# Fox queries and keys and the convolution's input turned by VectorE squares and memory, branches taken mixer by mixer, in a decoder layer on one Trainium2 core

## The chip, the core and the metric

The kernel runs on one core of one Trainium2 chip. The metric is device time in microseconds, the median of three runs. Engines are named as in the profile: PE (TensorE, matrix products; PEld is its weight load), DVE (VectorE), ACT (ScalarE), POOL (GpSimd), SP (SyncE). Transfers are issued from SP's queue (weights and other loads) and from POOL's (everything written to memory and read back).

## The reference, cut

One decoder layer over 256 tokens of 2048 channels in float32. One input product feeds three mixers; each mixer's output is multiplied by a weight matrix and by a gate, and the three are summed.

```python
u = rms_norm(x, attn_norm)
proj = einsum('bsd,de->bse', u, w_in)                    # 2048 -> 14424 columns
fq, fk, fv, ff, cq, ckv, kpe, gqkv, gz, gb, ga, gate = split(proj)
o_fox = fox_mixer(fq, fk, fv, ff, fox_fgate_bias)        # 8 heads of 128, causal, c_t - c_s on the logits
o_mla = mla_mixer(cq, ckv, kpe, ...)                     # 8 heads
def gdn_mixer(qkv, z, b_logit, a_logit, conv_w, ...):
    qkv_c = silu(causal_depthwise_conv(qkv, conv_w))     # 4 taps along the tokens, 3072 channels
    q, k, v = split(qkv_c); q, k = l2_norm(heads(q)), l2_norm(heads(k))
    o = gated_delta_rule_chunked(q, k, v, g, beta)       # a triangular solve in each chunk of 64
    return rms_norm(o, out_norm) * silu(z)
gates = sigmoid(gate)                                    # 3 x 2048 columns
merged = sum(gates[b] * einsum('bsc,cd->bsd', o[b], w_branch[b]) for b in range(3))   # fox, mla, gdn
x = x + einsum('bsd,de->bse', merged, w_out)
h = rms_norm(x, mlp_norm)
x = x + einsum('bsf,fd->bsd', square(relu(einsum('bsd,df->bsf', h, w_up))), w_down)
return rms_norm(x, final_norm)
```

## The kernel before

**Products.** `gemm` (L237) streams each weight matrix once, in steps. In a step SP loads two blocks of 128 rows by 512 columns into `raw` (four buffers), ACT rounds them to `wh` (L253), DVE forms the remainder `wl` (L254; three buffers each), and PE runs 12 matmuls (L260 to L262: two row blocks, two halves of the tokens, three products of high and low parts). A block of 512 output columns takes 8 steps where 2048 rows are summed, 4 in a branch (1024 rows). Where `evac` is called, the finished PSUM pair `mm` is read out, scaled by `scaled_evac` on ACT and DVE by turns.

**Order.** Each engine runs its instructions in the order written. `weave` runs one piece of a side generator behind every step: the mixers' own work is written as generators with `yield`s. `behind` keeps such a piece after the step's `wh` and `wl`. `later(k, f)` runs `f` k steps on; `tick` counts the steps. So a piece that waits holds up the next `wh` on ACT or the next `wl` on DVE, and through them PE.

**Two ways of turning.** A product needs its left operand with channels on partitions, and PSUM results have tokens there. Fox queries and keys (`fox_evac`, tile `ft`, L621) and the convolution's input (`gqkv_evac`, tile `cv`, L697) are transposed by PE into PSUM, 4 transposes of 128 by 128 for each half of the tokens and 512 columns. Then ACT and DVE copy `ft` to `fqT` and `fkT`; the convolution reads `cv` directly (one ACT operation L699 and three DVE operations L701 for each 128 channels). The branches' sum, the residual and the MLP's hidden layer instead go through `turned` (L1060 to L1065): two DVE transposes of 32 by 32 squares, one DMA that writes `turn` to memory, four that read it back permuted into `zy`, all five on POOL's queue, the four behind a wait for the first; TURN steps later ACT and DVE form high and low parts (`halves_of`, L1074 and L1075; behind w_out `gained`, L1124, ahead of them).

**Stages.** Latents; fox columns (six blocks) with the mla mixer woven in; the fox mixer; convolution columns (six blocks) with the delta rule's decays; the gate columns (96 steps) with the rest of the delta rule; the branches; w_out; four chunks of w_up and w_down. The forget gate's chain (softplus on DVE, tiles `sfp` and `nl`) ends in the small product `fc` (L640), followed by the mla products `bf` (L503 to L505). The delta rule's decay matrix `E` is read back from memory in one DMA (L1002's queue), worked on at L777 to L779, and multiplied with products `pg` into `AT` and `E` (L828 to L832). Its triangular solve runs on DVE in 31 rounds (tile `fs`, L853 and L855), goes to memory as `td`, comes back in eight DMAs as `DT`, is transposed by DVE into `D` (L878), and feeds small matmuls `pO` and `pD` (L886). In the branches the loop runs over four blocks n of 512 columns, and in each over the mixers in the order gdn, fox, mla; the sum `acc` of each n is turned at once. `load_x2` loads the residual at the start of w_out.

Of the kernel before, what the change touches and what calls it, by code (L numbers as in the profile page):

```python
# [11 lines left out]
F32 = mybir.dt.float32  # L12
# [6 lines left out]
P = 128  # L19
# [15 lines left out]
TURN = 9  # L35
# [22 lines left out]
def decoder_kernel(ctx: ExitStack, tc: tile.TileContext, x, attn_norm, w_in, fox_fgate_bias, mla_q_norm,  # L58
# [279 lines left out]
    def ev_copy(o, i):  # L338
        evc[0] += 1
        if evc[0] % 2:  # L340
            A.copy(out=o, in_=i)
        else:
            V.tensor_copy(out=o, in_=i)

# [263 lines left out]
    fv = big("fv").rearrange("p (t c) -> p t c", t=2)  # L608

# [3 lines left out]
    def fox_evac(bi, t, ps):  # L613
        if bi >= 4:
            scaled_evac(fv[:, t, (bi - 4) * 512:(bi - 3) * 512], ps, t)
            return
        e = me("fe")
        scaled_evac(e, ps, t)
        pt = psx("ft").rearrange("p (a t) -> p a t", a=4)
        for a in range(4):  # L620
            PE.transpose(pt[:, a, :], e[:, a * P:(a + 1) * P], ident)  # L621
        h0 = (bi % 2) * 4
        if bi < 2:
            A.activation(out=fqT[:, h0:h0 + 4, t * P:(t + 1) * P], in_=pt, func=AF.Copy, scale=-(HD ** -0.5))
        else:
            ev_copy(fkT[:, h0:h0 + 4, t * P:(t + 1) * P], pt)
# [58 lines left out]
    def gqkv_evac(bi, t, ps):  # L685
        e = me("gq")
        scaled_evac(e, ps, t)
        gx[t] = e
        if t == 0:
            return  # L690
        for a in range(2):
            pt = psx("cv").rearrange("p (a b) -> p a b", a=2)
            y = t2("y").rearrange("p (a b) -> p a b", a=2)
            for b in range(2):
                c = 2 * a + b
                for tt in range(2):
                    PE.transpose(pt[:, b, tt * P:(tt + 1) * P], gx[tt][:, c * P:(c + 1) * P], ident)  # L697
                ct = bi * 4 + c
                A.activation(out=y[:, b, :], in_=pt[:, b, :], func=AF.Copy, scale=cw[:, 72 + ct:73 + ct])  # L699
                for d in range(1, 4):  # L700
                    V.scalar_tensor_tensor(out=y[:, b, d:], in0=pt[:, b, 0:S - d],  # L701
                                           scalar=cw[:, (3 - d) * 24 + ct:(3 - d) * 24 + ct + 1],
                                           in1=y[:, b, d:], op0=ALU.mult, op1=ALU.add)
            ct = bi * 4 + 2 * a
            if ct < 16:
                h = ct % 8
                A.activation(out=kq[h // 4][:, h % 4:h % 4 + 2, 1 - ct // 8, :], in_=y, func=AF.Silu)
            else:
# [22 lines left out]
    def gdn():  # L731
# [53 lines left out]
        yield "decays"  # L785

# [257 lines left out]

    o_b = [[], [], o_gdn]
    again = [reload(spilled["fox"], "of", o_b[0]), reload(spilled["mla"], "om", o_b[1])]
    weave(gates(0, 12), chain(delta, *again))
    run(delta)

    def turned(src, then):

        zy = big("zy")
        z, y = zy[:, 0:1024], zy[:, 1024:2048]
        zv = z.rearrange("p (j t k b) -> p t k j b", j=4, t=2, k=4)
        for t in range(2):
            V.transpose(out=zv[:, t], in_=src[t].rearrange("p (k j b) -> p k j b", k=4, j=4))  # L1060
        d = dp.tile([P, 1024], F32, tag="turn", name=nm("turn"), bufs=4)
        nc.gpsimd.dma_start(out=d, in_=z)  # L1062
        dv = d.rearrange("(g a) (j x) -> j a g x", a=32, j=4)
        for j in range(4):
            nc.gpsimd.dma_start(out=y[32 * j:32 * j + 32].rearrange("a (g x) -> a g x", g=4), in_=dv[j])  # L1065
        later(TURN, lambda: then(y))

# [10 lines left out]
    for n in range(4):  # L1078
        acc = [t2("acc") for _ in range(2)]
        for i, b in enumerate((2, 0, 1)):  # L1080
# [4 lines left out]
            def evac(bi, t, ps, n=n, acc=acc, i=i, gt=gt):  # L1085
                g = gt[t]
                if i == 0:
                    V.tensor_tensor(out=acc[t], in0=ps, in1=g, op=ALU.mult)
                else:
                    V.tensor_tensor(out=g, in0=ps, in1=g, op=ALU.mult)  # L1090
                    V.tensor_tensor(out=acc[t], in0=acc[t], in1=g, op=ALU.add)
                if i == 2 and t == 1:
                    turned(acc, lambda y: halves_of(y, n, mHt, mLt))

            if n == 0 and b < 2:
                run(again[b])
            weave(gemm(by_tile(lambda k, b=b: o_b[b][0][:, k, :]), by_tile(lambda k, b=b: o_b[b][1][:, k, :]), w_branch[0, b], 0, 8,
                       [(n * 512, 512)], evac), chain(*again))
# [127 lines left out]
```

## Time and profile before

| | us |
|---|---|
| time, median of 3 runs | 1696.25 (1693.98 to 1700.75) |
| time of the profiled execution | 1696.24 |
| its span | 1694.5 |
| PE busy | 1672.8 (99%) |
| DVE busy | 1027.7 (61%) |
| ACT busy | 807.7 (48%) |
| POOL busy | 113.2 (7%) |

The profiled execution takes 1.7 us more than its span. PE is busy nearly throughout; its matmuls are pipelined, so busy does not mean at full rate, and time is also lost where they follow each other more slowly than elsewhere. Over the span the core moves 210 GB/s.

### The profile page before, as it was taken

How to read it: one execution, taken by the hardware profiler on the slowest of the kernel's cores; microseconds unless marked ns; L12 is line 12 of the kernel's file. 1: busy time of each engine (PE TensorE's matmuls, PEld its weight loads, DVE VectorE, ACT ScalarE, POOL GpSimd, SP SyncE). 2: the span in 40 equal slices, each digit the busy share in tenths (PEclk: the TensorE clock that was granted, in tenths of full speed). 3: DMA queues.
4: the chain of work that ended last, by engine and by line, in shares of the span. 5: the costliest groups of instructions: out<-in, count | busy, mean ns of one | idle time of the engine just before them, and what ended most of it. 6: DMA issues, size and time to landing. Idle time of an engine off the chain costs nothing.

```text
span 1694.5 us, 21459 instructions
## 1 busy us (share of the span) xinstructions
PE 1672.8 (99%) x7987; PEld 1403.8 (83%) x7987; DVE 1027.7 (61%) x1418; ACT 807.7 (48%) x1029; POOL 113.2 (7%) x202
## 2 busy tenths in 40 slices
PE   9999999999999999999999999999999999999997
PEld 9888889978788788888888778888888888888886
DVE  5746446676668845746675656555665556556655
ACT  6545436555646433544444554434443344434443
POOL 0000000000011100001210111100110011001100
PEclk9999999999999999999999999999999999999999
DMA  7755564766557755877888787856885687668863
GB/s 239 204 149 186 162 176 131 229 188 186 165 171 217 212 155 146 274 220 239 276 290 262 234 237 237 251 196 190 245 267 194 196 238 241 198 194 232 243 207 138
DMA packets 190761, 356.52 MB, mean 210 GB/s; under 512 B 17945, under 2 KB 38849, under 8 KB 190145
## 3 DMA queue, kind: packets, MB, share of 16 engines
q1 hardware_dynamic: 177040, 311.33, 60.7%
q0 software_dynamic: 13296, 43.29, 8.4%
q8 instruction: 62, 1.02, 0.2%
q10 hardware_dynamic: 320, 0.53, 0.1%
q14 instruction: 43, 0.34, 0.1%
HBM read 331.50 MB, written 23.61 MB: 210 GB/s over the span
## 4 chain that ended last, share of the span: by engine, by line
PE 93%; DMA 3%; DVE 2%; issue 1%; ACT 1%; POOL 0%; SPq 0%; DVEq 0%; POOLq 0%; ACTq 0%
PE mm L261 28%; PE mm L262 27%; PE mm L260 27%; DVE wl L254 1%; DMA raw<-in_w_in_dram 1%; DMA E<-gcd 1%; DMA raw<-in_w_up_dram 1%; PE bf L503 0%; PE bf L504 0%; PE bf L505 0%; PE mm L1188 0%; PE mm L1187 0%; PE mm L1186 0%; PE po L419 0%; PE pg L828 0%
## 5 line engine op out<-in xcount | busy, mean ns | idle before, releaser
L254 DVE TENSOR_TENSOR wl<-raw,wh 128x1024 fp32r<-128x1024 f32 (+3 forms) x552 | 663.4, 1203 | 542.7 <-ACT wh L253 539.9
L253 ACT CAST wh<-raw 128x1024 fp32r<-128x1024 f32 (+3 forms) x552 | 571.5, 1037 | 707.7 <-PE mm L262 647.6
L261 PE MATMUL mm<-wl,uH 128*128 128x512 f32 (+3 forms) x896 | 345.7, 386 | 1.6 <-DVE wl L254 1.6
L262 PE MATMUL mm<-wh,uL 128*128 128x512 f32 (+3 forms) x896 | 343.4, 383 | 0.0
L260 PE MATMUL mm<-wh,uH 128*128 128x512 f32 (+3 forms) x896 | 319.4, 387 | 2.6 <-ACT wh L253 2.6
L261 PE MATMUL mm<-wl,hH 128*128 128x512 f32 x512 | 199.4, 389 | 1.0 <-DVE wl L254 1.0
L262 PE MATMUL mm<-wh,hL 128*128 128x512 f32 x512 | 199.2, 389 | 0.0
L261 PEld LDWEIGHTS mm<-wl,uH 128*128 128x128 f32 x896 | 169.1, 189 | 33.2 <-DVE wl L254 3.6
L260 PEld LDWEIGHTS mm<-wh,uH 128*128 128x128 f32 x896 | 168.1, 189 | 32.9 <-ACT wh L253 3.1
L262 PEld LDWEIGHTS mm<-wh,uL 128*128 128x128 f32 x896 | 169.1, 189 | 29.6
L261 PE MATMUL mm<-wl,dH 128*128 128x512 f32 x480 | 186.7, 389 | 0.0
L262 PE MATMUL mm<-wh,dL 128*128 128x512 f32 x480 | 186.7, 389 | 0.0
L260 PE MATMUL mm<-wh,hH 128*128 128x512 f32 x512 | 178.5, 389 | 0.2 <-ACT wh L253 0.2
L260 PE MATMUL mm<-wh,dH 128*128 128x512 f32 x480 | 167.2, 389 | 0.0
L261 PEld LDWEIGHTS mm<-wl,hH 128*128 128x128 f32 x512 | 96.1, 188 | 21.8 <-DVE wl L254 1.9
L260 PEld LDWEIGHTS mm<-wh,hH 128*128 128x128 f32 x512 | 96.0, 188 | 20.5 <-ACT wh L253 0.6
L262 PEld LDWEIGHTS mm<-wh,hL 128*128 128x128 f32 x512 | 96.1, 188 | 19.9
L262 PEld LDWEIGHTS mm<-wh,dL 128*128 128x128 f32 x480 | 90.1, 188 | 18.7
L261 PEld LDWEIGHTS mm<-wl,dH 128*128 128x128 f32 x480 | 90.1, 188 | 18.7
L260 PEld LDWEIGHTS mm<-wh,dH 128*128 128x128 f32 x480 | 90.1, 188 | 18.7
L1065 POOL DMA_DIRECT2D zy<-turn x96 | 52.4, 553 | 104.7 <-DMA turn<-zy 31.5
L1062 POOL DMA_DIRECT2D turn<-zy x24 | 13.3, 556 | 643.0 <-DVE zy L1060 643.0
(419 smaller groups left out, 1754.5 us busy)
## 6 DMA issues: line engine op xcount, KB each, us to landing
raw<-in_w_in_dram SPq DMA_DIRECT2D x192, 512.0 KB, 4.0
raw<-in_w_up_dram SPq DMA_DIRECT2D x128, 512.0 KB, 4.3
raw<-in_w_down_dram SPq DMA_DIRECT2D x128, 512.0 KB, 4.4
raw<-in_w_branch_dram SPq DMA_DIRECT2D x48, 512.0 KB, 4.8
raw<-in_w_out_dram SPq DMA_DIRECT2D x32, 512.0 KB, 5.8
turn<-zy POOLq DMA_DIRECT2D x24, 512.0 KB, 3.3
zy<-turn POOLq DMA_DIRECT2D x96, 128.0 KB, 6.0
gd<-ge POOLq DMA_DIRECT2D x24, 256.0 KB, 4.7
```

The source lines that it names most:

```text
L253: h = A.copy(out=wh[:, :, :n], in_=raw[:, :, :n])
L254: l = V.tensor_tensor(out=wl[:, :, :n], in0=raw[:, :, :n], in1=wh[:, :, :n].bitcast(F32), op=ALU.subtract)
L260: PE.matmul(ps[t][:, :n], lhsT=lhsH(k, t), rhs=wh[:, kk, :n], start=(k == 0), stop=False)
L261: PE.matmul(ps[t][:, :n], lhsT=lhsH(k, t), rhs=wl[:, kk, :n], start=False, stop=False)
L262: PE.matmul(ps[t][:, :n], lhsT=lhsL(k, t), rhs=wh[:, kk, :n], start=False, stop=last)
L1062: nc.gpsimd.dma_start(out=d, in_=z)
L1065: nc.gpsimd.dma_start(out=y[32 * j:32 * j + 32].rearrange("a (g x) -> a g x", g=4), in_=dv[j])
```

## The change

The fox queries and keys and the convolution's input now go through `turned`, ten more groups of it; the 80 PE transposes `ft` and `cv` and their copies out of PSUM are gone. `turned` takes several functions, run on successive steps from step TURN on (8 instead of 9): for fox two `fox_heads` on ACT, for the convolution `by_channel` (two copies into `ch`) and two halves of `conv`, which now reads memory tile `ch` instead of PSUM. `tick` no longer keeps the first-in order of what is due. The delta rule waits 11 more steps behind its decays, and the reloads of the fox and mla outputs run beside it from step 80 on instead of behind it. The branches' outer loop is now over the mixers (fox, mla, gdn), the inner one over n; `acc` is one tile for all columns, and only the gdn pass turns it.

```diff
-TURN = 9
+TURN = 8
@@ tick
-        while pending and pending[0][0] <= 0:
+        due = [p for p in pending if p[0] <= 0]
+        pending[:] = [p for p in pending if p[0] > 0]
+        for p in due:
             with behind():
-                pending.pop(0)[1]()
+                p[1]()
@@ turned, moved up from behind the gates, and used by all
-    def turned(src, then):
+    def turned(src, *then, delay=TURN):
         zy = big("zy")
...
-        later(TURN, lambda: then(y))
+        for i, f in enumerate(then):
+            later(delay + i, lambda f=f: f(y))
@@ fox_evac
-        e = me("fe")
+        e = fe[t] = me("fe")
         scaled_evac(e, ps, t)
-        pt = psx("ft").rearrange("p (a t) -> p a t", a=4)
-        for a in range(4):
-            PE.transpose(pt[:, a, :], e[:, a * P:(a + 1) * P], ident)
+        if t == 1:
+            turned([fe[0], fe[1]], *[lambda y, t=t: fox_heads(bi, y, t) for t in range(2)])
+
+    def fox_heads(bi, y, t):
         h0 = (bi % 2) * 4
-        if bi < 2:
-            A.activation(out=fqT[:, h0:h0 + 4, t * P:(t + 1) * P], in_=pt, func=AF.Copy, scale=-(HD ** -0.5))
-        else:
-            ev_copy(fkT[:, h0:h0 + 4, t * P:(t + 1) * P], pt)
+        d = (fqT if bi < 2 else fkT)[:, h0:h0 + 4, t * P:(t + 1) * P].rearrange("p k (g b) -> p k g b", b=32)
+        yt = y.rearrange("p (g t k b) -> p t k g b", g=4, t=2, k=4)[:, t]
+        A.activation(out=d, in_=yt, func=AF.Copy, scale=-(HD ** -0.5) if bi < 2 else 1.0)
@@ gqkv_evac
-        for a in range(2):
-            pt = psx("cv").rearrange("p (a b) -> p a b", a=2)
...
-                    PE.transpose(pt[:, b, tt * P:(tt + 1) * P], gx[tt][:, c * P:(c + 1) * P], ident)
...
+        turned([gx[0], gx[1]], lambda y: by_channel(y, bi), lambda y: conv(y, bi, 0), lambda y: conv(y, bi, 1))
+
+    def by_channel(y, bi):
+        u = chans[bi] = big("ch")[:, 0:1024].rearrange("p (k t) -> p k t", k=4)
+        yv = y.rearrange("p (g t k b) -> p t k g b", g=4, t=2, k=4)
+        for t in range(2):
+            ev_copy(u[:, :, t * P:(t + 1) * P].rearrange("p k (g b) -> p k g b", b=32), yv[:, t])
+
+    def conv(_, bi, a):
...
@@ gdn, behind the decays
         yield "decays"
+        for _ in wait(11):
+            yield
@@ gates and branches
-    weave(gates(0, 12), chain(delta, *again))
-    run(delta)
+    mixers = both(delta, chain(idle(80), *again))
+    weave(gates(0, 12), mixers)
+    run(again[0])
...
-    for n in range(4):
-        acc = [t2("acc") for _ in range(2)]
-        for i, b in enumerate((2, 0, 1)):
+    acc = [big("acc") for _ in range(2)]
+    for b in range(3):
+        if b == 1:
+            run(again[1])
+        if b == 2:
+            run(mixers)
+        for n in range(4):
...
-                if i == 2 and t == 1:
-                    turned(acc, lambda y: halves_of(y, n, mHt, mLt))
+                if b == 2 and t == 1:
+                    turned([acc[tt][:, n * 512:(n + 1) * 512] for tt in range(2)], lambda y: halves_of(y, n, mHt, mLt))
...
-                       [(n * 512, 512)], evac), chain(*again))
+                       [(n * 512, 512)], evac), mixers)
```

Where the instructions stand now is shown at three places. `wl` of successive steps tell the steps apart.

**DVE, end of the triangular solve, before:** `NT` is the solve's result, from which `td` is written to memory, and `D` is the transposes of `DT`, which comes back.

```order
L855 TENSOR_REDUCE NT_939_4510<-fs_952_4589 128x16
L254 TENSOR_TENSOR wl_1068_5275<-raw_1066_5272,wh_1067_5274 128x1024
L254 TENSOR_TENSOR wl_1075_5301<-raw_1073_5298,wh_1074_5300 128x1024
L254 TENSOR_TENSOR wl_1080_5325<-raw_1078_5322,wh_1079_5324 128x1024
L878 STREAM_TRANSPOSE D_1076_5316<-DT_1042_5134 32x16x32 x2
L254 TENSOR_TENSOR wl_1083_5343<-raw_1081_5340,wh_1082_5342 128x1024
L878 STREAM_TRANSPOSE D_1076_5316<-DT_1042_5134 32x16x32
L254 TENSOR_TENSOR wl_1088_5397<-raw_1086_5394,wh_1087_5396 128x1024
```

After, the same place:

```order
L888 TENSOR_REDUCE NT_982_4724<-fs_999_4811 128x16
L256 TENSOR_TENSOR wl_1086_5333<-raw_1084_5330,wh_1085_5332 128x1024
L256 TENSOR_TENSOR wl_1090_5355<-raw_1088_5352,wh_1089_5354 128x1024
L256 TENSOR_TENSOR wl_1093_5373<-raw_1091_5370,wh_1092_5372 128x1024
L256 TENSOR_TENSOR wl_1096_5399<-raw_1094_5396,wh_1095_5398 128x1024
L256 TENSOR_TENSOR wl_1099_5417<-raw_1097_5414,wh_1098_5416 128x1024
L256 TENSOR_TENSOR wl_1102_5435<-raw_1100_5432,wh_1101_5434 128x1024
L256 TENSOR_TENSOR wl_1109_5461<-raw_1107_5458,wh_1108_5460 128x1024
L256 TENSOR_TENSOR wl_1112_5479<-raw_1110_5476,wh_1111_5478 128x1024
L256 TENSOR_TENSOR wl_1115_5497<-raw_1113_5494,wh_1114_5496 128x1024
L256 TENSOR_TENSOR wl_1118_5515<-raw_1116_5512,wh_1117_5514 128x1024
L911 STREAM_TRANSPOSE D_1119_5530<-DT_1087_5350 32x16x32 x3
```

Three `wl` stood between the solve and `D`, now there are ten.

**DVE, the branches' sum, before:** the `zy` transposes of n=0, and the low halves `mL` that read what comes back; `gate` and `acc` are the read-out of the next products.

```order
L1060 STREAM_TRANSPOSE zy_1385_6946<-acc_1335_6700 128x4x4x32
L1060 STREAM_TRANSPOSE zy_1385_6946<-acc_1336_6701 128x4x4x32
L254 TENSOR_TENSOR wl_1404_7020<-raw_1402_7017,wh_1403_7019 128x1024
L254 TENSOR_TENSOR wl_1411_7046<-raw_1409_7043,wh_1410_7045 128x1024
L254 TENSOR_TENSOR wl_1414_7064<-raw_1412_7061,wh_1413_7063 128x1024
L1088 TENSOR_TENSOR acc_1387_6955<-mm_1391_6961,gate_1389_6957 128x512
L1088 TENSOR_TENSOR acc_1388_6956<-mm_1392_6962,gate_1390_6958 128x512
L254 TENSOR_TENSOR wl_1417_7082<-raw_1415_7079,wh_1416_7081 128x1024
L254 TENSOR_TENSOR wl_1420_7100<-raw_1418_7097,wh_1419_7099 128x1024
L254 TENSOR_TENSOR wl_1427_7128<-raw_1425_7125,wh_1426_7127 128x1024
L1075 TENSOR_TENSOR mL_1333_6698<-zy_1385_6946,mH_1331_6696 128x4x128 x2
```

After, in the gdn pass (the two `zy` transposes of n=0 stand just above the first row; those of n=1 are among the rows):

```order
L256 TENSOR_TENSOR wl_1504_7512<-raw_1502_7509,wh_1503_7511 128x1024
L256 TENSOR_TENSOR wl_1513_7549<-raw_1511_7546,wh_1512_7548 128x1024
L256 TENSOR_TENSOR wl_1516_7567<-raw_1514_7564,wh_1515_7566 128x1024
L1123 TENSOR_TENSOR gate_1489_7449<-mm_1491_7453,gate_1489_7449 128x512
L1123 TENSOR_TENSOR gate_1490_7450<-mm_1492_7454,gate_1490_7450 128x512
L1124 TENSOR_TENSOR acc_1341_6708<-acc_1341_6708,gate_1489_7449 128x512
L1124 TENSOR_TENSOR acc_1342_6709<-acc_1342_6709,gate_1490_7450 128x512
L256 TENSOR_TENSOR wl_1519_7585<-raw_1517_7582,wh_1518_7584 128x1024
L356 STREAM_TRANSPOSE zy_1505_7531<-acc_1341_6708 128x4x4x32
L356 STREAM_TRANSPOSE zy_1505_7531<-acc_1342_6709 128x4x4x32
L256 TENSOR_TENSOR wl_1522_7603<-raw_1520_7600,wh_1521_7602 128x1024
L1103 TENSOR_TENSOR mL_1339_6706<-zy_1487_7440,mH_1337_6704 128x4x128 x2
```

Six `wl` stood between `zy` and `mL`, now five, and the next group's `zy` stands ahead of them. ACT's cast `mH` of the same group stands at the same step.

**ACT, end of w_out and start of w_up, before:** `wh` casts, and `gcol`, the scaling of what comes back from memory for the third block of columns (n=2).

```order
L253 CAST wh_1665_8380<-raw_1664_8378 128x1024
L253 CAST wh_1695_8443<-raw_1694_8441 128x1024
L1124 ACTIVATE zy_1639_8233<-zy_1639_8233,gcol_92 128x8x32 x4
L253 CAST wh_1698_8469<-raw_1697_8467 128x1024
L253 CAST wh_1701_8487<-raw_1700_8485 128x1024
L1116 ACTIVATE junk_1667_8397,ss2_1550_7738<-xx0_1543_7732 128x512
L1074 CAST hH_1546_7735<-zy_1639_8233 128x4x128 x2
```

After:

```order
L255 CAST wh_1662_8364<-raw_1661_8362 128x1024
L255 CAST wh_1665_8382<-raw_1664_8380 128x1024
L1155 ACTIVATE zy_1639_8243<-zy_1639_8243,gcol_92 128x8x32 x4
L255 CAST wh_1695_8453<-raw_1694_8451 128x1024
L1102 CAST hH_1546_7733<-zy_1639_8243 128x4x128 x2
L255 CAST wh_1698_8471<-raw_1697_8469 128x1024
```

The scaling of n=2 stood behind the first cast of w_up, now it stands behind the last cast of w_out, one step earlier.

## Rows read from the trace of the kernel before

**Rows 1.** Of the page: busy time of each engine with its share of the span and its instructions, and the chain that ended last, its shares by engine:

```profile
PE 1672.8 (99%) x7987; PEld 1403.8 (83%) x7987; DVE 1027.7 (61%) x1418; ACT 807.7 (48%) x1029; POOL 113.2 (7%) x202
...
PE 93%; DMA 3%; DVE 2%; issue 1%; ACT 1%; POOL 0%; SPq 0%; DVEq 0%; POOLq 0%; ACTq 0%
```

**Rows 2.** What TensorE waited for, over the whole span: engine, line and releaser, us in total, times, longest us:

```profile
PE fc L640 <- issue: 2.8, 1, 2.8
...
PE pO L886 <- DVE D L878: 0.7, 1, 0.7
```

**Rows 3.** Five stretches of the span: us, then busy us and (instructions) of each engine, granted TensorE clock as a share of full speed, busy share of the DMA engines, GB/s:

```profile
84.00:92.00 8.00, 5.23 (x33) 5.02 (x32) 3.72 (x12) 3.35 (x7) 0.00 (x0) 0.79 0.46 134
356.00:376.00 20.00, 16.27 (x70) 12.27 (x69) 14.55 (x35) 11.46 (x16) 0.00 (x0) 1.00 0.54 175
584.00:611.00 27.00, 25.90 (x235) 20.56 (x234) 11.12 (x12) 9.28 (x11) 5.60 (x10) 0.87 0.65 198
700.00:825.00 125.00, 125.00 (x553) 103.42 (x552) 71.06 (x72) 56.94 (x61) 14.58 (x27) 1.00 0.80 250
960.00:1000.00 40.00, 37.74 (x162) 29.80 (x161) 23.65 (x38) 21.57 (x34) 5.47 (x10) 1.00 0.70 210
```

**Rows 4.** The two groups of TensorE transposes, over the span (count, duration in ns min/median/max, first and last start), a piece of one of them in the chain of work (start us, us, what), and one of the four-matmul pieces of `pg`, which the sum needs further on:

```profile
L697 PE MATMUL cv<-cst,gq x48: 270/272/328, 346.6 to 525.9; 128*128 128x128 f32 x48
...
L621 PE MATMUL ft<-cst,fe x32: 270/272/417, 87.5 to 221.5; 128*128 128x128 f32 x32
...
163.19 0.87 PE ft L621 x8
...
500.96 0.86 PE pg L828 x4
```

**Rows 5.** The chain of work around the forget gate's prefix sum `fc`: start us, us, what:

```profile
84.31 2.75 issue
...
87.65 1.24 PE ft L621 x8
...
88.89 0.21 PE bf L503
```

**Rows 6.** VectorE's groups over the span, shapes apart: line, operation, out<-in, shapes, count | busy us, mean ns of one | idle time before them and its releaser:

```profile
L254 DVE TENSOR_TENSOR wl<-raw,wh 128x1024 fp32r<-128x1024 f32 x520 | 635.1, 1223 | 517.4 <-ACT wh L253 516.7 <-DMA om<-om_d 0.3
...
L1060 DVE STREAM_TRANSPOSE zy<-acc 128x512 f32<-128x512 f32 x8 | 5.2, 689 | 0.0
...
L701 DVE SCALAR_TENSOR_TENSOR y<-cv,cw,y 128x255 f32<-128x255 f32 x24 | 11.0, 478 | 2.4 <-ACT y L699 2.3
...
L830 DVE TENSOR_TENSOR AT<-pg,E 128x256 f32<-128x256 f32 x8 | 3.3, 420 | 1.6 <-PE pg L828 1.5
...
L832 DVE SCALAR_TENSOR_TENSOR E<-pg,ns,E 128x128 f32<-128x128 f32 x16 | 4.8, 345 | 0.2
...
L175 DVE TENSOR_TENSOR rnt<-rnt,rnh 128x32 f32<-128x32 f32 x3 | 0.6, 186 | 0.0
```

**Rows 7.** The chain of work where the delta rule's `DT` is made and its first small matmuls run (start us, us, what); the last line is VectorE's waits of 584 to 611 us:

```profile
580.55 3.92 DMA td<-NT
...
585.65 4.18 DMA DT<-td
...
594.65 0.43 PE mm L261
...
608.14 0.43 PE mm L262
...
DVE D L878 <- DMA DT<-td: 5.5, 1, 5.5
```

**Rows 8.** The chain of work where `E` is read back (start us, us, what), and TensorE's instructions behind it (start us, us, instruction, idle before it and releaser):

```profile
352.31 9.02 DMA E<-gcd
...
365.52 0.74 PE L260 MATMUL mm<-wh,uH 128*128 128x512 f32 x2 [2.65 <-ACT wh L253]
```

**Rows 9.** ScalarE's instructions at the end of the w_out product: start us, us, instruction, idle before it and releaser:

```profile
962.32 1.71 ACT L1124 ACTIVATE zy<-zy,gcol 128x256 f32<-128x256 f32 x4 [3.37 <-DMA zy<-turn]
...
986.75 1.71 ACT L1124 ACTIVATE zy<-zy,gcol 128x256 f32<-128x256 f32 x4 [4.52 <-DMA zy<-turn]
```

**Rows 10.** GpSimd's DMA issues in the branches and at the start of w_out (start us, us, instruction, idle before it and releaser), and, last, the SyncE issues of the residual `xx`:

```profile
869.94 0.54 POOL L1062 DMA_DIRECT2D turn<-zy  x1 [19.13 <-DVE zy L1060]
...
874.74 2.21 POOL L1065 DMA_DIRECT2D zy<-turn  x4 [4.26 <-DMA turn<-zy]
...
902.58 0.54 POOL L1062 DMA_DIRECT2D turn<-zy  x1 [23.48 <-DVE zy L1060]
...
911.38 2.21 POOL L1065 DMA_DIRECT2D zy<-turn  x4 [8.26 <-issue]
...
945.16 0.56 POOL L1062 DMA_DIRECT2D turn<-zy  x1
...
955.70 1.10 POOL L1065 DMA_DIRECT2D zy<-turn  x2 [2.10 <-issue]
...
898.16 4.55 SPq L1106 DMA_DIRECT2D xx<-in_x_dram  x6
```

**Rows 11.** Of the page, DMA issues: out<-in, queue, count, KB each, median us from issue to landing:

```profile
turn<-zy POOLq DMA_DIRECT2D x24, 512.0 KB, 3.3
...
zy<-turn POOLq DMA_DIRECT2D x96, 128.0 KB, 6.0
```

More of the change, by code (lines that the diff above doesn't have):

```diff
@@ L343, in ev_copy @@
             V.tensor_copy(out=o, in_=i)
+    def turned(src, *then, delay=TURN):
+        zy = big("zy")
+        z, y = zy[:, 0:1024], zy[:, 1024:2048]
+        zv = z.rearrange("p (j t k b) -> p t k j b", j=4, t=2, k=4)
+        for t in range(2):
+            V.transpose(out=zv[:, t], in_=src[t].rearrange("p (k j b) -> p k j b", k=4, j=4))
+        d = dp.tile([P, 1024], F32, tag="turn", name=nm("turn"), bufs=4)
+        nc.gpsimd.dma_start(out=d, in_=z)
+        dv = d.rearrange("(g a) (j x) -> j a g x", a=32, j=4)
+        for j in range(4):
+            nc.gpsimd.dma_start(out=y[32 * j:32 * j + 32].rearrange("a (g x) -> a g x", g=4), in_=dv[j])
+        for i, f in enumerate(then):
+            later(delay + i, lambda f=f: f(y))
     cw_r = cp.tile([96, P], F32, tag="cw_r", name="cw_r")
@@ L608, in decoder_kernel @@
     fv = big("fv").rearrange("p (t c) -> p t c", t=2)
+    fe = {}
     def fox_evac_at(b0):
@@ new lines, in gqkv_evac @@
+        turned([gx[0], gx[1]], lambda y: by_channel(y, bi), lambda y: conv(y, bi, 0), lambda y: conv(y, bi, 1))
+    chans = {}
+    def by_channel(y, bi):
+        u = chans[bi] = big("ch")[:, 0:1024].rearrange("p (k t) -> p k t", k=4)
+        yv = y.rearrange("p (g t k b) -> p t k g b", g=4, t=2, k=4)
+        for t in range(2):
+            ev_copy(u[:, :, t * P:(t + 1) * P].rearrange("p k (g b) -> p k g b", b=32), yv[:, t])
+    def conv(_, bi, a):
+        u = chans[bi]
+        y = t2("y").rearrange("p (a b) -> p a b", a=2)
+        for b in range(2):
+            c = 2 * a + b
+            ct = bi * 4 + c
+            A.activation(out=y[:, b, :], in_=u[:, c, :], func=AF.Copy, scale=cw[:, 72 + ct:73 + ct])
+            for d in range(1, 4):
+                V.scalar_tensor_tensor(out=y[:, b, d:], in0=u[:, c, 0:S - d],
+                                       scalar=cw[:, (3 - d) * 24 + ct:(3 - d) * 24 + ct + 1],
+                                       in1=y[:, b, d:], op0=ALU.mult, op1=ALU.add)
+        ct = bi * 4 + 2 * a
+        if ct < 16:
+            h = ct % 8
+            A.activation(out=kq[h // 4][:, h % 4:h % 4 + 2, 1 - ct // 8, :], in_=y, func=AF.Silu)
+        else:
+            h = ct - 16
+            A.activation(out=y, in_=y, func=AF.Silu)
+            pb = psx("vb").rearrange("p (t b d) -> p t b d", t=2, b=2)
+            for tt in range(2):
+                for b in range(2):
+                    PE.transpose(pb[:, tt, b, :], y[:, b, tt * P:(tt + 1) * P], ident)
+            ev_copy(vtok[:, :, h * P:(h + 2) * P], pb.rearrange("p t b d -> p t (b d)"))
@@ L1043, in reload, with idle, both @@
                 yield
+    def idle(n):
+        for _ in wait(n):
+            yield
+    def both(*gens):
+        gens = list(gens)
+        while gens:
+            gens = [g for g in gens if next(g, gens) is not gens]
+            yield
     o_b = [[], [], o_gdn]
     again = [reload(spilled["fox"], "of", o_b[0]), reload(spilled["mla"], "om", o_b[1])]
-    weave(gates(0, 12), chain(delta, *again))
-    run(delta)
-    def turned(src, then):
[L1056 to L1065, printed above, removed]
-        later(TURN, lambda: then(y))
+    mixers = both(delta, chain(idle(80), *again))
+    weave(gates(0, 12), mixers)
+    run(again[0])
     def halves_of(y, n, H, L):
```

33 lines of the change are left out of this document (5 added, 28 removed).

## The prediction

> **What bounds the kernel now.** I read the busy times first: PE is busy for 1672.8 of 1694.5 us and makes up 93% of the chain that ended last [rows 1]. The list of what PE waited for holds little, its largest entry 2.8 us ahead of `fc` [rows 2]. So I looked for time that PE loses without being listed, by stretches. From 700 to 825 us it runs 553 matmuls in 125 us, 0.226 us each, so a step of 12 takes 2.71 us: PE at full rate [rows 3]. Four stretches fall short: 84 to 92 (idle 2.8), 356 to 376 (idle 3.7), 584 to 611 (idle 1.1, granted clock 0.87) and 960 to 1000, where 162 matmuls should take 36.6 us and take 40 [rows 3]. A change pays if it takes work off PE or shortens one of these, and it costs if it makes a fifth. The other engines have room on the whole (DVE 61%) [rows 1]. Only their local order can stop PE: `wl` runs ahead of PE by its three buffers, some two steps or 5.4 us.
>
> **PE's work that goes.** The 80 transposes have the same duration in both groups, median 272 ns, but that is latency: eight of them take 0.87 us in the chain, 0.109 each [rows 4]. The first eight of `ft` belong to `fc`, below. The other 72 are worth **−7.8 us**, since PE bounds where they stand.
> [...]
>
> **The stretch at `fc`.** PE waits 2.75 us, then runs eight `ft` (1.24 us), and `bf` starts at 88.89 [rows 5]. The wait ends with DVE's softplus chain. The two new transposes of the fox block, 0.689 us each [rows 6], stand in that chain, so `fc` comes at least 1.4 us later, and up to 2.1 if the remainders that change places there also come first. The 1.24 us go. So `bf` starts 0.2 to 0.9 us later: **+0.6**.
>
> **The triangular solve.** Of `td`'s 3.92 us and `DT`'s 4.18 us, DVE waited 5.5 us ahead of `D` [rows 7]; the `wl` behind it were late for PE. [...] The half clock comes in two stretches, matmuls of 0.43 us around 594 (behind the wait) and around 608 (behind `pD`'s small matmuls) [rows 7]. The first stretch and the idle time, 1.75 + 1.1, belong to the wait. Now ten steps, 27 us, lie between the solve and `D` instead of three, against some 9.3 us of transfers. So **−2.9**; nothing if another transfer delays `DT`, −4.6 if the second stretch goes too.
>
> **The stretch at `E`.** `E` takes 9.02 us to come back and PE idles 2.65 us behind it [rows 8]. This chain stays. There are ten `cv` transposes less for PE ahead of it, 1.1 us, which lengthen the wait, and some convolution operations (0.478 us each [rows 6]) less on DVE within it. The turn of the first convolution block is queued behind `E` on POOL, so `ch` may be late. I take **0**, between −1.5 and +2.
>
> **The convolution's last block on DVE.** Its halves ran right behind its product; now they come six to eight steps later, among the norm (16 small operations of 0.186), `AT` (0.420) and `E` (0.345) [rows 6]. Between four `wl` I count on DVE: 4 `wl` 4.9, norm 3.0, six `AT` 2.5, ten `E` 3.5, a copy 0.7 (as a transpose), ten convolution operations 4.8; together 19.4 us. PE has four steps, 10.8, and two pieces `pg` of 0.86 [rows 4], 12.6 in all. The excess of 6.8 against a lead of 5.4 leaves 1.4 late; as the steps ahead are full too, the lead is not whole. **+2**, between 0 and +4. Convolution operations read memory now instead of PSUM; I keep their price, and half of it would end this term.
>
> **The end of w_out.** ACT waits twice for `zy` there, 3.37 and 4.52 us [rows 9]. The second wait, n=2, moves one step earlier, ahead of a cast that was hidden; what it waits for starts no earlier. **+2.7**, one step; 0 if `zy` lands a step earlier.
>
> **The branches.** In the gdn pass a block is turned every 4 steps instead of 12, and what comes back must be there in 5 steps instead of 6: 13.6 us instead of 16.3, plus what ACT is ahead, at most half a us by my estimate. A chain from the issue of `turn` to the last landing, with the median 6.0 us of `zy` [rows 11], took 13.0 us at 869.94 and 17.0 at 902.58, when the residual's loads ran at 898.16 to 902.71; one that overlapped another took 17.6 from 945.16 [rows 10]. Before, all fitted, as PE lost nothing from 700 to 825. Now the residual's loads meet the third block: about 3 us late for it, others hardly. **+2**, between 0 and +8.
>
> **What costs nothing.** Ten more groups of `turned` put 20 × 0.689 = 13.8 us on DVE, spread over 300 us in which PE is the bound; 50 more DMA issues go to POOL, busy 7%. The fox blocks wait eight, then six steps, more than a chain of 13. The `acc` reads and sums are as many as before. If that cover fails, one late chain costs what it is late, 1 to 4 us.
>
> **Sum.** −7.8 + 0.6 − 2.9 + 0 + 2 + 2.7 + 2 = −3.4 us. The profiled execution took 1696.24, the median of runs is 1696.25, so the difference carries over: **1692.8 us**. What a measurement of this kernel can tell from no change is about 0.5%, 8.5 us: faster means under 1687.8, slower over 1704.7.
>
> **Rivals.**
> *All covers hold:* no new wait in the convolution, w_out and branches. −7.8 + 0.2 − 2.9 = −10.5, 1685.7 (to 1682.5 if the second clock stretch and `E` gain too). For it: DVE's 61%, and no loss from 700 to 825. Against: the two waits of [rows 9] are there already.
> *New waits take the gain:* `E` +2, the convolution +4, w_out 2.7, the branches +4, and 0.9 at `fc`; −7.8 − 2.9 + 13.6 = +2.9, 1699.1.
> *Slower:* the overlapping chains of the gdn pass. If three of them take 17.6 plus 0.3 to the issue, as the overlapping one did, each is late 3.8 against 14.1, 11.4 instead of my 2, and behind each stop PE runs a stretch at half clock (1.75, as at 594): −5.4 + 11.4 + 5.2 = +11.2, 1707.4. It decides from about 17 us in all three. For it: turns follow each other at 10.9 us, less than a chain; against: only the last of four chains in the branches was that long.
> [...]
> *Transposes at their duration:* 72 × 0.272 instead of × 0.109 takes 11.7 us more off, 1681.1; the piece of 0.87 us for eight speaks against it.
>
> **Chances.** Forecast (1688 to 1696.5) 0.44, all covers hold 0.24, new waits 0.20, slower 0.10, transposes at duration 0.02. Faster 0.26, same 0.64, slower 0.10. The range, 1684 to 1701, leaves out the slower rival and the far end of the fast ones.
>
> **What would show it.** PE matmuls without `ft` and `cv`, and no half-clock stretch behind the first `pO`; `fc` idle of 4 us or more; DVE full where `AT` is made, PE waiting on `wl` there; ACT waiting on `zy` in the gdn pass and at the last cast of w_out. Wrong would be: `D` still waiting, chains over 17 us in the gdn pass, or no wait at any of the places where I put one.

## Result and the profile after

The changed kernel takes 1700.12 us (median of 20 runs, 1696.84 to 1707.12), the kernel before 1694.87 in the same comparison: a ratio of 1.0037, 95% interval 1.0028 to 1.0046. By the ratio that is some 6.3 us slower (5.3 by the two medians), where 3.4 us faster was forecast. The time lies within the prediction's range, 1684 to 1701, and the change is under 0.5%; the sign is wrong.

The profiled execution took 1703.49 us, 3.4 more than the median; its span is 1701.7 us, 7.2 more than before. Of the page after, the lines that answer to [rows 1]:

```profile
PE 1669.0 (98%) x7907; PEld 1397.5 (82%) x7907; DVE 1042.4 (61%) x1442; ACT 807.0 (47%) x1035; POOL 141.4 (8%) x252
...
PE 78%; issue 10%; DMA 7%; DVE 3%; ACT 1%; POOL 1%; SPq 0%; DVEq 0%; ACTq 0%; POOLq 0%
```

The 80 transposes are gone and PE is busy 3.8 us less, yet the chain that ended last lies on PE for 78% of the span instead of 93%; 10% is now "issue" and 7% DMA. What PE waited for, as in [rows 2] (engine, line and releaser, us in total, times, longest us):

```profile
PE mm L262 <- ACT wh L255: 10.0, 5, 2.9
PE mm L263 <- DVE wl L256: 4.8, 9, 0.7
PE fc L662 <- issue: 4.1, 1, 4.1
...
PE pn L832 <- ACT sqH L828: 1.2, 1, 1.2
```

The waits for `wh` and `wl` have grown from 6.5 to 14.8 us. To place them I compared the start of the same product step in both traces. The table gives by how much a stage came to be longer (+) or shorter in the changed kernel, beside the prediction's terms for it:

| Stage (before, us) | Forecast | In the traces |
|---|---|---|
| latents, fox columns (to 263), with the stretch at `fc` | −2.0 | −2.1 |
| convolution columns and what hangs on them (320 to 540) | −3.2 | +4.3 |
| rest of the gate columns, the triangular solve (540 to 724) | −2.9 | −3.9 |
| gdn pass and start of w_out (887 to 925) | +2 | +4.3 |
| end of w_out, start of w_up (925 to 999) | +2.7 | +3.7 |
| all else | 0 | +0.9 |
| sum | −3.4 | +7.2 |

Each line compares one execution with one. The first, third and fifth are near what was forecast; how much of that is the execution's own is told further down. The miss of 10.6 us is the convolution's stage, 7.5 of it.

**The convolution's stage after.** ACT's waits from 340 to 500 us in the changed kernel:

```profile
ACT ch L343 <- DMA zy<-turn: 24.5, 5, 7.8
```

Five of ACT's six copies into `ch` (DVE makes six more) waited for data, 24.5 us in all. The forecast had such a wait as possible for the first block alone, and that is the one that did not wait. One of the five, with ACT's read-out of half that block, the cast ahead of the copy and the one behind it (ACT's timeline: start us, us, instruction, idle before it and releaser):

```profile
388.55 0.68 ACT L336 ACTIVATE gq<-mm,rstd 128x512 f32<-128x512 f32 x1
...
402.16 1.05 ACT L255 CAST wh<-raw 128x1024 fp32r<-128x1024 f32 x1 [1.62 <-PE mm L264]
411.00 0.62 ACT L343 COPY ch<-zy 128x512 f32<-128x512 f32 x1 [7.78 <-DMA zy<-turn]
411.52 1.04 ACT L255 CAST wh<-raw 128x1024 fp32r<-128x1024 f32 x1
```

The next `wh` cast came at 411.52 instead of some 405. ACT stood 7.8 us, and PE, two steps behind it, ran dry: it waited 2.33 us for that cast and 0.53 us for the `wl` behind it. DVE ahead of that chain shows why the data were late:

```profile
390.38 1.26 DVE L732 SCALAR_TENSOR_TENSOR y<-ch,cw,y 128x253 f32<-128x253 f32 x3
391.57 0.74 DVE L338 TENSOR_SCALAR gq<-mm,rstd 128x512 f32<-128x512 f32 x1
392.23 0.70 DVE L356 STREAM_TRANSPOSE zy<-gq 128x512 f32<-128x512 f32 x1
392.85 1.18 DVE L256 TENSOR_TENSOR wl<-raw,wh 128x1024 fp32r<-128x1024 f32 x1
393.96 0.87 DVE L732 SCALAR_TENSOR_TENSOR y<-ch,cw,y 128x254 f32<-128x254 f32 x2
394.74 0.70 DVE L356 STREAM_TRANSPOSE zy<-gq 128x512 f32<-128x512 f32 x1
```

The two `zy` squares of one block start at 392.23 and 394.74: a `wl` and two operations of the previous block's convolution stand between them. Three more of these operations stand just ahead of `gq`, DVE's read-out of the block's other half, which starts 3.0 us behind ACT's. One transfer writes both; it was issued at 395.7 us, behind the second square, and the last of the four that read it back landed at 410.9.

### The profile page after: what moved, and what is told of

Read it like the earlier page. It is cut to its first block, busy times and chain, and to the rows that moved or that the text cites. A ratio compares the mean times of both kernels' runs of the same rounds, so it can differ in the third digit from the quotient of the medians.

```text
span 1701.7 us, 21428 instructions
## 1 busy us (share of the span) xinstructions
PE 1669.0 (98%) x7907; PEld 1397.5 (82%) x7907; DVE 1042.4 (61%) x1442; ACT 807.0 (47%) x1035; POOL 141.4 (8%) x252
## 4 chain that ended last, share of the span: by engine, by line
PE 78%; issue 10%; DMA 7%; DVE 3%; ACT 1%; POOL 1%; SPq 0%; DVEq 0%; ACTq 0%; POOLq 0%
PE mm L263 23%; PE mm L264 23%; PE mm L262 23%; DMA zy<-turn 4%; DMA turn<-zy 2%; DVE wl L256 1%; POOL zy L361 1%; DMA raw<-in_w_out_dram 1%; DVE y L732 1%; ACT wh L255 1%; PE bf L523 0%; PE bf L525 0%; PE bf L524 0%; PE mm L1219 0%; PE mm L1218 0%
## 5 line engine op out<-in xcount | busy, mean ns | idle before, releaser
L262 PEld LDWEIGHTS mm<-wh,dH 128*128 128x128 f32 x480 | 90.0, 188 | 18.8 <-ACT wh L255 0.2
L264 PEld LDWEIGHTS mm<-wh,dL 128*128 128x128 f32 x480 | 90.1, 188 | 18.6
L361 POOL DMA_DIRECT2D zy<-turn x136 | 74.5, 555 | 150.8 <-issue 54.2
L358 POOL DMA_DIRECT2D turn<-zy x34 | 19.0, 558 | 798.5 <-DVE zy L356 689.8
```

The costliest lines, as they stand in the source:

```text
L262: PE.matmul(ps[t][:, :n], lhsT=lhsH(k, t), rhs=wh[:, kk, :n], start=(k == 0), stop=False)
L264: PE.matmul(ps[t][:, :n], lhsT=lhsL(k, t), rhs=wh[:, kk, :n], start=False, stop=last)
```

## Experiments

All ratios are to the kernel before on the same chip; the changed kernel has 1.0037 [1.0028, 1.0046]. 0.1% is 1.7 us. The changed kernel was not measured again beside them, so a difference between two ratios carries both intervals, some 2.5 to 3 us together: a smaller one cannot be told from none.

**1. Convolution two steps later.**

```diff
-        turned(..., lambda y: by_channel(y, bi), lambda y: conv(y, bi, 0), lambda y: conv(y, bi, 1))
+        turned(..., lambda y: by_channel(y, bi), lambda y: conv(y, bi, 0), lambda y: conv(y, bi, 1), delay=TURN + 2)
-        for _ in wait(11):
+        for _ in wait(13):
```

> The changed kernel with the convolution's three functions run two steps later (delay TURN+2 for them alone, and the delta rule's 11 steps of waiting made 13 so that it still comes behind them). Theory A, the conv chains come back too late: ACT's and DVE's waits for zy ahead of ch (7.8 us at 411, up to 5.7 at 461) fall under 1 us each, PE's losses of about 5 us at 407 to 418 and of about 5 us at 450 to 470 go, and the time falls by 5 to 9 us, to 1691 to 1695. Rival B, DVE is overfull with squares, convolution and norm there: the waits for zy go too, but the work only moves on, and the time stays within 2 us of 1700 or rises.

Measured: 0.9973 [0.9962, 0.9984], 10.8 us below the changed kernel, more than theory A's 5 to 9, and 4.6 below the one before. ACT's waits ahead of `ch` are gone. Theory A holds against rival B: the same operations are on DVE, and PE no longer waits for them (from 384 to 424 us it runs 178 matmuls, as in run 2 below). It does not say whether the copies or the convolution had stood wrongly, since both moved.

**2. Copies in place, convolution two steps later.** This separates the two.

```diff
-        turned(..., lambda y: by_channel(y, bi), lambda y: conv(y, bi, 0), lambda y: conv(y, bi, 1))
+        turned(..., lambda y: by_channel(y, bi), lambda y: None, lambda y: None, lambda y: conv(y, bi, 0), lambda y: conv(y, bi, 1))
-        for _ in wait(11):
+        for _ in wait(13):
```

> The changed kernel with the two halves of the convolution two steps later, but the copies into ch at the step where they stand in the change. Theory A1, what counts is that ch is copied before the data can be back: ACT's wait ahead of ch stays (over 4 us twice or more), and the time falls by 3 us at most. Theory A2, the convolution's operations stand between the next block's two squares on DVE and hold the second one up, so that the next chain starts late: with them gone the squares stand 0.7 us apart instead of 3.2, the chains shorten, and most of the 9 us goes: 1691 to 1694.

Measured: 0.9987 [0.9976, 0.9998], 8.5 us below the changed kernel. ACT's wait at the copies, and ACT's read-out and DVE's timeline at the same block:

```profile
ACT ch L343 <- DMA zy<-turn: 2.0, 1, 2.0
```

```profile
387.25 0.69 ACT L336 ACTIVATE gq<-mm,rstd 128x512 f32<-128x512 f32 x1 [0.98 <-PE mm L264]
...
387.94 0.75 DVE L338 TENSOR_SCALAR gq<-mm,rstd 128x512 f32<-128x512 f32 x1 [0.41 <-PE mm L264]
388.60 1.29 DVE L356 STREAM_TRANSPOSE zy<-gq 128x512 f32<-128x512 f32 x2
389.82 1.18 DVE L256 TENSOR_TENSOR wl<-raw,wh 128x1024 fp32r<-128x1024 f32 x1
390.93 1.26 DVE L732 SCALAR_TENSOR_TENSOR y<-ch,cw,y 128x255 f32<-128x255 f32 x3
```

The copies stand at the same step as in the changed kernel, yet wait 2.0 us instead of 24.5. The two squares are one piece now, and the convolution comes behind them. A2 holds: what made the data late was the convolution's place on DVE, not the step of the copies. It stood ahead of the squares as well as between them. From the start of ACT's read-out to the end of the second square it took 6.9 us in the changed kernel (388.55 to 395.44) and 2.6 here (387.25 to 389.89); of the difference 2.3 us lie ahead of the first square and 1.9 between the two. The four transfers that read this block back were slower too; their time to landing, in the changed kernel and here:

```profile
DMA to landing us min/median/max: 5.8/7.2/8.3
```

```profile
DMA to landing us min/median/max: 3.3/3.4/5.3
```

Why they took longer there stays open. Both runs also let the delta rule wait 13 steps; in the changed kernel its work behind that wait starts with ACT's `sq` at 443.95, later than the first three of the five waits (2.4, 7.8 and 6.0 us), so it did not cause those. The two stretches from 384 to 424 us (us, busy us and instructions of each engine, granted clock, DMA share, GB/s), first the changed kernel, then this one:

```profile
384.00:424.00 40.00, 37.15 (x155) 29.93 (x155) 28.29 (x45) 20.44 (x29) 3.30 (x6) 0.96 0.70 202
```

```profile
384.00:424.00 40.00, 40.00 (x178) 33.10 (x177) 31.26 (x47) 23.98 (x32) 5.50 (x10) 1.00 0.84 250
```

PE runs 155 matmuls in 40 us against 178: 23 at 0.226 us are 5.2 us, in this stretch alone. Of them PE stood idle for 2.85, and the granted clock of 0.96 over 40 us lost 1.6.

**3. Convolution's input transposed by TensorE again**, fox, branches and the 11 steps of waiting as in the change (`gqkv_evac` of the kernel before).

> The changed kernel with the convolution's input transposed by TensorE again, as before; the 11 steps of waiting stay, fox and branches as in the change. Theory A: both conv waits go (about -9), 48 transposes of 0.109 us come back (+5.2), so -3 to -5 us, 1695 to 1697. Theory B gives the same here. If the loss came from the fox part or the branches, no change or +5.

Measured: 1.0032 [1.0020, 1.0044], not what was expected: no gain over the changed kernel that can be told. In the trace the convolution's stage is shorter by 6.7 us than in the changed kernel, which is more than expected, but the 3.9 us of the triangular solve's stage are gone and the branches lose 2 more. PE's wait says where:

```profile
PE pO L910 <- DMA DT<-td: 1.9, 1, 1.9
```

`DT` is late again: three `wl` stand between the solve and `D`, as before, and ten in the changed kernel, though the 11 steps of waiting are in both. The solve ends at 602.9 us here, at 588.2 in the changed kernel. So this stage hangs on the convolution's part; how that part moves the end of the solve is not shown.

**4. Fox queries and keys transposed by TensorE again** (`fox_evac` of the kernel before).

> The changed kernel with the fox queries and keys transposed by TensorE again, convolution and branches as in the change. The prediction's terms: 24 transposes of 0.109 us come back (+2.6), the stretch at fc gets 0.6 us shorter; +2 us, 1701 to 1703. Rival: the fox turns cost DVE and ACT time that PE waits for, and the time falls, by 1 to 2 us.

Measured: 1.0065 [1.0049, 1.0082]: 4.7 us above the changed kernel, more than the forecast's +2, and the interval reaches down to 2. Idle time at `fc` is 2.8 us again. The sign of the fox part's term is right. In the traces the stage with the fox columns is only 0.6 us longer than in the changed kernel, but the granted clock from 84 to 94 us is 1.00 here and 0.83 there, worth 1.7 us. How much of the rest is the convolution's, whose waits came to 26.3 us here, stays open.

**5. w_out's blocks used 9 steps on, as before.**

```diff
-            turned([x2[tt][...] for tt in range(2)], lambda y: gained(y, n))
+            turned([x2[tt][...] for tt in range(2)], lambda y: gained(y, n), delay=TURN + 1)
```

> The changed kernel with w_out's turned blocks used 9 steps on instead of 8, as before. Theory A, the one-step-earlier wait for zy of n=2 costs a step: -2.7 to -3.5 us, ACT's wait of 7.1 us at 989 falls to some 4.5. Rival: that wait ends when the transfer lands, whatever stands behind it, and the loss only moves: within 1 us.

Measured: 1.0022 [1.0009, 1.0035], −2.5 us, which is near theory A but cannot be told from none. ACT's waits for `zy` from 955 to 1005, the changed kernel and this one:

```profile
ACT zy L1155 <- DMA zy<-turn: 10.0, 2, 7.1
```

```profile
ACT zy L1155 <- DMA zy<-turn: 8.1, 2, 4.9
```

The longer wait falls as theory A said. In the trace the end of w_out is 3.4 us shorter, and most of that is the clock. From 985 to 1000 us, the changed kernel and this one (columns as in run 2):

```profile
985.00:1000.00 15.00, 12.08 (x41) 8.91 (x40) 8.39 (x14) 7.96 (x14) 0.56 (x1) 0.77 0.58 164
```

```profile
985.00:1000.00 15.00, 13.46 (x57) 10.20 (x56) 8.41 (x12) 8.13 (x15) 0.56 (x1) 1.00 0.69 185
```

**6. The residual's loads eight steps later** (`chain(idle(8), load_x2())`).

> The changed kernel with the residual's eight loads issued eight steps later in w_out, out of the gdn pass's last chains. Theory A, the loads make the chains of n=2 and n=3 late (16.1 and 18.9 us): chains of 13 to 15 us, ACT's wait of 6.8 us at 907 falls by 2 or more, -2 to -4 us. Rival, the chains are late because they follow each other every 4 steps: the waits stay, within 1 us. Either way the loads may fall on w_out's own first chain, +1 to +2.

Measured: 1.0046 [1.0028, 1.0063], no difference from the changed kernel that can be told. The theory falls: the chain of n=2 does get shorter, 14.3 us from issue to landing instead of 15.9, but ACT waits 13.8 us in the gdn pass with the loads elsewhere, 14.6 with them there. The chains there are late whether or not the residual is loaded.

**7. The gdn pass's blocks used a step later**, which needs w_out's order altered (`late` is 8 for w_out, where LATE is 12):

```diff
-            order.sort(key=lambda o: (max(o[0], 1), o[0] < 2 and o[1] >= LATE))
+            order.sort(key=lambda o: (max(o[0], 1), o[0] < 2 and o[1] >= late))
-                    turned([...], lambda y: halves_of(y, n, mHt, mLt))
+                    turned([...], lambda y: halves_of(y, n, mHt, mLt), delay=TURN + (n < 3))
```

> The changed kernel with the gdn pass's blocks n=0 to 2 used one step later (six steps behind their squares again), which w_out allows by taking its second block's rows from 8 on instead of 12 on last. Theory, the wait for zy one step too early costs the 4.5 us lost at 900 to 925: ACT's waits ahead of mH (14.6 us in all) fall below 7, -2 to -4 us. Rival, the weights' loads that crowd there are the bound (ACT waited 8.4 us for raw of w_out): the waits move to raw, within 1 us.

Measured: 0.9981 [0.9969, 0.9993], 9.5 us below the changed kernel, more than expected. ACT's waits from 860 to 930, the changed kernel and this one:

```profile
ACT mH L1102 <- DMA zy<-turn: 14.6, 3, 6.8
ACT wh L255 <- DMA raw<-in_w_out_dram: 8.4, 4, 3.3
```

```profile
ACT wh L255 <- DMA raw<-in_w_out_dram: 8.7, 4, 3.2
ACT mH L1102 <- DMA zy<-turn: 5.4, 2, 3.4
```

The wait for `zy` falls from 14.6 to 5.4 us, the weights' stays, so five steps were one too few. In the trace the gdn pass is 2.1 us shorter, and some 7 come off at the end of w_out, from the altered order (run 8).

**8. w_out's order alone.**

> The changed kernel with w_out's order alone altered: rows from 8 on, instead of from 12 on, of its first two blocks come last, nothing is used later. In the run that had this and the later use in the gdn pass, 5 us went in the gdn pass and 6 us at the end of w_out. If the order gives the second part, w_out's first two blocks end four steps apart instead of two and their chains stop crowding each other: -4 to -6 us, 1694 to 1696, with the gdn pass losing 4 to 5 us as before. If both came from the later use: within 1 us of 1700.

Measured: 1.0022 [1.0010, 1.0035], −2.5 us, less than the −4 to −6 expected and not to be told from none. In the trace the end of w_out is 7.2 us shorter than in the changed kernel's, and ACT's wait for `mH` in the gdn pass stays (16.7 us). So in the traces the two parts of run 7 are apart, the order at the end of w_out, the later use in the gdn pass. The time fell by less than that: this execution lost some 2 us more in the convolution's stage (27.6 us of waits at `ch`) and as much in the gdn pass. It was the slowest of its twelve; why the median gives no more stays open.

**9. The same order in the kernel before.**

> The kernel before with w_out's order alone altered in the same way. If the loss at the end of w_out belongs to the two chains that end two steps apart, it is there before too (3.4 us) and goes: -2 to -4 us. If it comes from the change: no difference.

Measured: 0.9995 [0.9982, 1.0009]. No difference that can be told, though ACT's wait for `zy` there falls from 7.9 to 2.3 us and the trace is 2.6 us shorter there. The interval allows up to 3 us, so whether the order helps the kernel before stays open; most of what it removes in run 7 is not there before.

**10. `DT` and `D` cleared by VectorE instead of GpSimd** (`V.memset`).

> The changed kernel with the two clearings of DT and D done by VectorE instead of GpSimd, at the same place in the program. In the changed kernel four VectorE operations at 482.0 to 486.0 us end together, 3.8 us long instead of 0.18 and 0.42, while GpSimd clears DT and D (482.33 to 485.90). Theory: GpSimd's clearing holds VectorE up. Then the long operations are gone, PE gains 2 to 4 us at 484 to 496, and VectorE pays some 2 us where it has room: 1697 to 1699. Rival: VectorE was held by something else, and its operations stay at 3.8 us; no change.

Measured: 1.0045 [1.0028, 1.0062]. The long operations are gone, so the theory of what held VectorE is right; the rows are in the last section. The time did not fall: it is 1.4 us above the changed kernel, which cannot be told from none. In this trace the convolution's waits were the longest of all (30.9 us); what the hold costs in time stays open.

**11. Three mends together**: runs 1, 5 and 7.

> The changed kernel with three mends together: the convolution's functions two steps later, the gdn pass's and w_out's turned blocks one step later. If the losses are apart: about -10 (convolution), -1.5 (w_out), -3 (gdn pass), 1685 to 1688. If they hang together (what one gives, the next takes): no better than 1690, the time with the convolution alone mended.

Measured: 1683.01 us, 0.9926 [0.9912, 0.9940], 12.5 us faster than the kernel before. The losses are apart in the main: −10.8, −9.5 and −2.5 give −22.8 by themselves, together they brought −18.8. At the end of w_out this trace is 7.2 us shorter than the changed kernel's, and so is run 7's alone, so run 5's edit adds nothing to run 7's there; the rest of the difference lies within the intervals. This kernel has all the change's edits, and it is faster than the one before.

**12. The same, with the first fox block's squares two steps later** (`later(2, ...)` around `turned` for block 0).

> The kernel with three mends, and the squares of the first fox block two steps later, out of the softplus chain ahead of fc. The prediction's term: the idle time at fc goes from 4.1 back to 2.75 us, -1.3 us against the three mends alone (1683.0). Rival: the chain's end is set by the remainders that stand in it, and the idle time stays near 4; no difference.

Measured: 1680.36 us, 0.9932 [0.9920, 0.9944]: by the ratio the same as run 11. The idle time at `fc`, 4.0 us in run 11, is as forecast:

```profile
PE fc L667 <- issue: 2.8, 1, 2.8
```

So the two squares had cost 1.2 us there, which is no more than the interval hides.

## Why the prediction was wrong

**Where it failed.** The step is "What costs nothing": the ten added groups were put at 13.8 us of DVE time "spread over 300 us in which PE is the bound", and if cover failed, "one late chain costs what it is late, 1 to 4 us". The working looked for a collision on DVE only at the convolution's last block, where the norm also stands. But a block of columns is 8 steps, and functions 8 steps behind a block's squares fall on the next block's read-out and squares: the collision is at every block. By the order of the rows it also feeds itself, though no run tests that alone: late data make the copies late, which make the convolution late, which holds up the next block's squares, which makes the next data late. So the waits came to 24 to 31 us of ACT time in the changed kernel and in each of the six runs that left the convolution there, against none in run 1 and 2.0 in run 2. Five chains of six were late, by 2.4 to 7.8 us, where the prediction allowed for one. The stage cost 4.3 us where −3.2 was forecast; with the convolution moved it gave −5.6 and −6.3 (runs 1 and 2), which is the transposes' −5.2 and a little. The order of the instructions is the program's, so the squares stood apart in it before anything ran; the prediction read that order at three other places.

**PE's transposes** at 0.109 us each: right, by runs 1 and 2. The fox columns' −2.1 against −2.0 fits as well, but alone it shows little: nine other executions with the same code there gave −0.4 to −2.7. That they would bring 272 ns each is refuted: the convolution's 48 would then have brought 13.1 us.

**The convolution's last block**, +2: not tested at its own place. From 440 to 500 us PE is busy for 57.67 of 60 us in the changed kernel, but late data for `ch` are part of that. In run 2, where the block's convolution stands two steps later, PE is busy for all 60.

**`fc`**, +0.6: right in mechanism and size. Idle went from 2.75 to 4.1 us, and back to 2.8 in run 12.

**The triangular solve**, −2.9: the trace has −3.9, but the price of the wait was mis-sized. The term's 1.75 us of half clock are half of what the clock of 0.87 in [rows 3] loses, 0.13 of 27 us or 3.5 us, one half for each of its two stretches. In the trace before, the two are (columns as above):

```profile
590.00:600.00 10.00, 8.90 (x84) 6.59 (x84) 7.16 (x8) 2.67 (x3) 1.12 (x2) 0.83 0.71 215
604.00:612.00 8.00, 8.00 (x112) 6.99 (x112) 1.91 (x2) 2.63 (x4) 0.00 (x0) 0.79 0.49 133
```

Each loses 1.7 us by its clock, which is 0.50 from 593.5 to 596.5 and from 607.5 to 610 us. In the changed kernel the wait for `DT` is gone, and of these stretches (columns as above) the first two ran at full clock, without idle PE:

```profile
575.00:602.00 27.00, 27.00 (x121) 22.36 (x120) 20.09 (x21) 11.81 (x12) 6.10 (x11) 1.00 0.80 231
602.00:626.00 24.00, 24.00 (x148) 19.57 (x147) 11.97 (x12) 10.65 (x11) 1.13 (x2) 1.00 0.74 214
626.00:640.00 14.00, 14.00 (x155) 11.69 (x153) 4.95 (x5) 5.33 (x9) 1.08 (x2) 0.88 0.61 186
```

The third row is the stretch with the small matmuls of the delta rule's next part: its mean clock of 0.88 over 14 us is 3.4 us at half clock (0.12 of 14 us, doubled), and from 636 to 639 us it is 0.50. So of the half-clock stretches of [rows 7] the one behind the wait is gone, and the second is still there, as the sum assumed. But run 9 is a second execution of the code of before up to w_out. There PE's stretch of [rows 3] and VectorE's wait of [rows 7] are:

```profile
584.00:611.00 27.00, 26.16 (x256) 21.10 (x255) 11.98 (x13) 10.58 (x13) 5.62 (x10) 1.00 0.64 194
...
DVE D L878 <- DMA DT<-td: 5.3, 1, 5.3
```

The wait is the same and the clock does not fall; this execution is 3.7 us faster over the stage than the profiled one of before. And in runs 5, 7, 8 and 10, which have the changed kernel's code here, PE also runs at full clock throughout; they are 5.5 to 5.6 us faster. Without half clock on either side the stage gains some 1.9 us, not 2.9. The 1.75 us of half clock that the term laid to the wait come in one execution and not in another, with the wait there, so that −3.9 came near the term is partly luck.

**`E`**, 0: right. PE's wait behind it is 2.3 us instead of 2.65, and the changed kernel is 3.0 us ahead just before that wait and 3.3 behind it.

**The end of w_out**, +2.7: the wait is right, and that the trace's +3.7 is so near is partly luck. ACT's second wait of [rows 9] grew from 4.52 to 7.14 us:

```profile
988.88 1.70 ACT L1155 ACTIVATE zy<-zy,gcol 128x256 f32<-128x256 f32 x4 [7.14 <-DMA zy<-turn]
```

But the granted clock of 0.77 from 985 to 1000 us (rows in run 5; 0.50 from 991 to 997) lost 3.4 us, and the term had no half clock in it. In the five other executions with the same code at this place the stage gave +1.1 to +5.1 (runs 2 and 10 the ends), and the step given back in run 5 brought −2.5 us of time, not to be told from none.

**The gdn pass**, +2 with 0 to 8: mechanism right, +4.3, and its reason partly wrong. I laid it on the residual's loads; run 6 moved them and the wait stayed, run 7 gave the chains a step more and it fell. Five steps are 13.6 us, and the four chains took 13.5, 14.1, 15.9 and 18.6 us from the issue of `turn` to the last landing; ACT waited for three of them. So a chain is too long for five steps, with the residual's loads or without; the slower rival asked for 17 us in three of them, and one had it.

**The range** held the result by luck. It reached to the rival in which new waits take the gain, +2.9 us, but the largest wait was not among those it named, and the change is +6.3. From the forecast's own baseline of 1696.25 that is 1702.5, outside; the kernel before came out at 1694.87 in the comparison.

## What to carry to other kernels

When work is put a fixed number of steps behind its cause, look at what stands at that step in the next round of the loop, on every engine, before you price it by its sum: a delay equal to the loop's length puts the end of one round into the start of the next. Two operations that open a chain of transfers belong together; what stood ahead of them and between them here, 2.3 and 1.9 us in one block, delayed the whole chain, and the next round may hang on it. Before a gain read from one execution is credited to a term, look whether half-clock stretches come and go with the same code, as from 584 to 611 us in the kernel before and in run 9 (granted clock 0.87 and 1.00). Here moving the convolution by two steps turned 6.3 us of loss into 4.6 us of gain.

## What the runs showed of the hardware

GpSimd's clearing of memory (MEMSET) held VectorE, but not every VectorE operation. In the changed kernel (VectorE's, then GpSimd's timeline: start us, us, instruction):

```profile
482.02 3.93 DVE L167 TENSOR_SCALAR rni<-nrm 128x32 int32<-128x32 int32 x1
482.10 3.87 DVE L168 TENSOR_SCALAR rnh<-nrm 128x32 f32<-128x32 f32 x1
482.19 3.78 DVE L863 TENSOR_TENSOR AT<-pg,E 128x256 f32<-128x256 f32 x2
```

```profile
482.33 1.83 POOL L894 MEMSET DT<- 128x2048 f32 x1
484.07 1.83 POOL L908 MEMSET D<- 128x2048 f32 x1
```

Four VectorE operations (the third row holds two), which take 0.17 to 0.42 us elsewhere, end together at 485.95, with the end of the second MEMSET. In runs 5 to 8, with the same order, the first of them took 3.92 to 4.15 us. With the clearing on VectorE (run 10) they are short:

```profile
487.84 0.17 DVE L167 TENSOR_SCALAR rni<-nrm 128x32 int32<-128x32 int32 x1
487.92 0.26 DVE L168 TENSOR_SCALAR rnh<-nrm 128x32 f32<-128x32 f32 x1
488.01 0.75 DVE L863 TENSOR_TENSOR AT<-pg,E 128x256 f32<-128x256 f32 x2
```

Before, the same two MEMSETs stood beside `wl` and `AT`, and these were not held (GpSimd's, then VectorE's):

```profile
488.78 1.82 POOL L861 MEMSET DT<- 128x2048 f32 x1
490.52 1.83 POOL L875 MEMSET D<- 128x2048 f32 x1
```

```profile
489.12 1.21 DVE L254 TENSOR_TENSOR wl<-raw,wh 128x1024 fp32r<-128x1024 f32 x1
490.25 0.75 DVE L830 TENSOR_TENSOR AT<-pg,E 128x256 f32<-128x256 f32 x2
```

In the changed kernel the two TENSOR_SCALAR operations took 3.6 to 3.8 us longer than in run 10, and the two `AT` behind them 3.78 us instead of 0.75. In the kernel before, beside the same MEMSETs, the TENSOR_TENSOR operations `wl` (1.21 us) and `AT` (0.75 us for two) were not held. So `AT` in the changed kernel was probably late only for standing behind the two TENSOR_SCALAR. Why these were held and the others not, no run shows.
